# First-layer modulation weights loaded by column quarters, with the first products following the quarters

## The chip, the cores and the metric

The kernel runs on one core of one Trainium2 chip. The metric is the device time of one execution in microseconds (us). Three executions of the kernel before took 2706.11, 2706.01 and 2699.67 us; their median is 2706.01 us.

## The reference, cut to what matters

The network has two layers over a sequence of 2048 tokens of width 1024. Everything is float32. The first layer is a gated linear attention with four heads; before it, the input is normed and modulated by a condition vector `c`:

```
cond        = silu(c) @ w_ada[0] + b_ada[0]            # w_ada[0]: 1024 x 3072
shift, scale, gate = split(cond, 3)                    # 1024 each
h           = rms_norm(x, norm_gain[0]) * (1 + scale) + shift
q,k,v,g,lr  = split(h @ gla_w_in[0])                   # the first products
gk          = log_sigmoid(lr @ w_gk2 + b_gk) / 16      # the decay of each head
x           = x + gate * gla(q, k, v, g, gk) @ gla_w_out[0]
```

The second layer is a stick-breaking attention with sixteen heads whose keys and values come from the first layer's output; a last norm follows. The change touches only the calculation of `shift` and `scale` of the first layer and the first products that use them.

## The kernel before, in words

Channels lie on the 128 partitions and tokens along the free dimension. A block of 1024 channels is eight k-tiles (`KT` = 8), and the tokens are four groups of 512 (`TG`). Layer 0 goes over the groups (`layer0`). For each group it calculates `h` for eight k-tiles, and then for each head `v` (`pv`, two halves of two 128-token blocks), the key and the query (`pk`, `pq`), the decays (`gate`), the chunked attention (`gla`), and the output projection. A float32 value is held as a high and a low part in a form that TensorE multiplies in one pass, so each product is three matmuls: high by high, high by low, low by high. Weights are split the same way: ScalarE copies the high part (L116) and VectorE subtracts for the low part (L117).

TensorE's order is the order in which the program is written. The other engines are ordered by a planner, except in `start()`, which is written inside a region (L668) where TensorE, ScalarE, VectorE and SyncE all keep the written order too. The planner may put instructions of the rest of the program between those of the region.

`start()` is the work up to the first group's `h`. It loads `x` in four transfers and squares it on ScalarE; it loads `w_ada[0]`, columns 0 to 2047, as sixteen tiles of 128 rows by 1024 columns (`ada_rows`, L235), each multiplied by a column of silu(c) and added up on VectorE (L242, L244). Six of these come before the norm's `rstd` (L214) in VectorE's order and ten behind it. GpSimd multiplies `x` by `rstd` (L323). When all sixteen are added, TensorE sums them over partitions with sixteen one-column matmuls (L250), VectorE adds the bias and forms `1 + scale` times the gain (L331, L271), and for each k-tile `h` is scaled and shifted (GpSimd, VectorE or ScalarE, L338 and L341) and split (L230, L231). The split of the gate's low-rank weights (L371 to L375) and of the first `v` weights stands in front of that.

Behind `start()`, `gate_low_rank` (L378) multiplies each k-tile by the low-rank weights into `plr`, and the first half of the first head's `pv` runs between (L434 sorts it by k-tile). Its second half, `pk` and `pq` follow. The first head's `gate` is called four steps into what is left of `qkv`; it needs the finished `plr` (through `T.lr`), issues the matmul `u` (L395) and then a chain of VectorE and ScalarE instructions (L399 to L425), whose results are multiplied by `pk` (L457 to L460) and `pq` (L464, L465). The first attention matmul, `psc` (L474), needs the products of L457 and L464. It is written six steps behind the end of `qkv` of its head, between the `pv` matmuls of the next head.

Accumulation banks come from small pools: `pl` has four banks and holds `ms`, `plr`, `pv`, `pk`, `pq` and `u`; `pw` has two. The pool `act` has twelve tiles of 4 KB per partition (`w_ada` tiles and the first four k-tiles of `h` are among them), `wraw` three for unsplit weights and `wsp` ten for split ones.

Of the kernel before, what the change touches and what calls it, by code (L numbers as in the profile page):

```python
# [9 lines left out]
F32 = mybir.dt.float32  # L10
# [24 lines left out]
def yoco_kernel(ctx: ExitStack, tc: tile.TileContext, I: dict, O: dict):  # L35
# [29 lines left out]
    def bank(pool, name):  # L65
        return pool.tile([P, 512], F32, tag=pool.name, name=name)
# [241 lines left out]
    def start():  # L308

        T = start_group(0)  # L310
        w = I["w_ada"][0]
        rows = [ada_rows("l0", w, j, act) for j in range(2)]
        xs, sq = [], []
# [15 lines left out]
        for j in range(2):
            ada_sum(pc[:, 8 * j:8 * j + 8], accs[j])  # L330
        nc.vector.tensor_tensor(cond, pc[:, 0:16], b_ada[:, 0:16], op=ALU.add)  # L331
        a, b = mods["l0m"] = modulation("l0", norm_gain[:, 0:8], cond)
        xn = [t2(f"xn_0_{kt}") for kt in range(KT)]

        def scaled(kt):
            s, t = a[:, kt:kt + 1], b[:, kt:kt + 1]
            if kt % 2 == 0 and kt:
                nc.scalar.activation(xn[kt], xs[kt], AF.Identity, bias=t, scale=s)  # L338
            else:
                eng = nc.vector if kt < 1 else nc.gpsimd  # L340
                eng.tensor_scalar(xn[kt], xs[kt], s, t, op0=ALU.mult, op1=ALU.add)  # L341

        scaled(0)
        for kt in range(KT):
            if kt + 1 < KT:
                scaled(kt + 1)
            h = new_h(0, kt)
            T.hs.append(split(h[:, 0], h[:, 1], xn[kt]))
        return T
# [15 lines left out]

    def gate_weights():
# [3 lines left out]
        nc.sync.dma_start(raw2, I["w_gk2"])  # L370
        with urgent():  # L371
# [3 lines left out]
            nc.vector.tensor_tensor(gk2[64:96], raw2[64:96], gk2[64:96].bitcast(F32), op=ALU.subtract)  # L375

    def gate_low_rank(T):
        pr = bank(po, f"plr_{T.g}")  # L378
        for kt in range(KT):
            nc.tensor.matmul(pr[0:32], lrw[:, kt], T.hs[kt][0], start=kt == 0, stop=False)  # L380
            nc.tensor.matmul(pr[0:32], lrw[:, kt], T.hs[kt][1], start=False, stop=kt == KT - 1)
            yield
# [45 lines left out]
    def qkv(T, h):  # L428

        n = f"{T.g}_{h}"  # L430
        wv = next_weight()
        v = t4(f"v_{n}", [P, 4, GV])
        for half in range(2):
            pv = bank(pl, f"pv_{n}_{half}")  # L434

            steps = [(kt, s) for s in range(2) for kt in range(KT)]
            if T.g == h == half == 0:
                steps.sort()
            for i, (kt, s) in enumerate(steps):
# [9 lines left out]
            with urgent():  # L449
                nc.scalar.activation(v[:, 2 * half:2 * half + 2], pv, AF.Copy)  # L450
        wkq = next_weight()
        G = T.G[h]
        G.v = v
        pk = bank(pl, f"pk_{n}")
        yield from mm3(pk, wkq, 0, T.hs)
        with urgent():
# [3 lines left out]
            nc.vector.tensor_tensor(G.kf, pk, G.kf, op=ALU.mult)  # L460
        pq = bank(pl, f"pq_{n}")
        yield from mm3(pq, wkq, 1, T.hs)
        with urgent():
# [141 lines left out]
    def weight_blocks():  # L605

        for g in range(NG):
            seq = [("v", 0), ("kq", 0), ("v", 1), ("kq", 1), ("v", 2), ("kq", 2), ("g", 0),
                   ("v", 3), ("kq", 3), ("g", 1), ("g", 2), ("g", 3)] + [("out0", i) for i in range(4)]
            for kind, i in seq:  # L610
                yield load_split(f"{kind}{g}_{i}", I["w_" + kind][i])
# [49 lines left out]
    def layer0():  # L661
# [4 lines left out]
        for g in range(NG):  # L666
            T.ready = 0
            first = qkv(T, 0)  # L668
            for _ in gate_low_rank(T):
                if g == 0:  # L670
                    next(first)
            spawn(slow, 1, 9)
# [400 lines left out]
```

## Time and profile before

| | before |
|---|---|
| median of three executions | 2706.01 us |
| the profiled execution, its own time | 2703.88 us |
| its span, first to last instruction | 2702.1 us |
| mean granted clock of TensorE, as a share of full speed | 0.989 |
| TensorE busy | 2607.2 us, 96% |
| VectorE busy | 2110.4 us, 78% |
| ScalarE busy | 1517.6 us, 56% |
| GpSimd busy | 167.4 us, 6% |
| mean DMA rate | 138 GB/s |

The span runs from the first to the last instruction; 1.8 us of the execution's own time lie around it. PE is TensorE's matmuls, PEld its weight loads, DVE is VectorE, ACT is ScalarE, POOL is GpSimd and SPq is the queue of transfers that SyncE issues. Matmuls are pipelined, so one that the profile shows as 0.28 us long can be followed by the next after 0.12 us; the distance of starts is the pace. The granted clock of 0.50 is 1.2 GHz and 1.00 is 2.4 GHz.

### The profile page before, as it was taken

The page shows a single profiled execution, that of the slowest core. Times are in us where ns is not written, and L with a number is a line of the kernel's source. Part 1 is how long each engine was busy: PE and PEld are TensorE (multiplying, and loading weights), DVE is VectorE, ACT ScalarE, POOL GpSimd, SP SyncE. Part 2 cuts the span into 40 slices and gives each one's busy share as a digit, 9 for nine tenths or more (in the row PEclk, how much of TensorE's full clock was granted, in tenths as well). Part 3 has the DMA queues.
Part 4 walks back from the last instruction along what each step waited for, and adds up shares of the span by engine and source line. Part 5 has one row for each costly group of instructions (what it writes and reads, how often), then busy time and mean ns, then how long its engine had stood idle before and what let it go on. Part 6 is the DMA issues. An engine that isn't in the chain of part 4 may idle for free.

```text
span 2702.1 us, 38165 instructions
## 1 busy us (share of the span) xinstructions
PE 2607.2 (96%) x14040; PEld 2184.4 (81%) x14040; DVE 2110.4 (78%) x2933; ACT 1517.6 (56%) x2677; POOL 167.4 (6%) x358
## 2 busy tenths in 40 slices
PE   5999999999999999999999999999999999999998
PEld 4888888888788878788787887887887887887887
DVE  7647767676675658978979969979879789789866
ACT  4746756574485445545545645546556555556644
POOL 3000000000000011000010010010000010010000
PEclk7999999999999999999999999999999999999999
DMA  6326445545732463342243334243243243323464
GB/s 246 118 74 209 151 151 175 168 148 173 232 131 72 164 247 127 106 145 90 96 146 116 114 107 154 88 137 116 75 148 110 72 151 113 115 93 117 148 212 147
DMA packets 116682, 371.91 MB, mean 138 GB/s; under 512 B 13872, under 2 KB 18096, under 8 KB 116496
## 3 DMA queue, kind: packets, MB, share of 16 engines
q1 hardware_dynamic: 116496, 369.47, 40.8%
q8 instruction: 111, 1.82, 0.3%
q14 instruction: 75, 0.61, 0.1%
HBM read 311.75 MB, written 40.89 MB: 131 GB/s over the span
## 4 chain that ended last, share of the span: by engine, by line
PE 75%; DVE 17%; ACT 3%; issue 3%; DMA 1%; POOL 0%; SPq 0%; DVEq 0%; POOLq 0%; ACTq 0%
PE pt L838 7%; DVE S L830 5%; PE z L822 4%; PE o L856 4%; PE z L821 4%; PE o L855 3%; DVE sl L842 3%; PE pg L150 2%; PE pg L152 2%; PE pg L151 2%; PE pf L150 2%; PE pf L151 2%; PE pf L152 2%; PE py L150 2%; PE lk L150 2%
## 5 line engine op out<-in xcount | busy, mean ns | idle before, releaser
L841 ACT ACTIVATE sh<-pt 128x512 fp32r<-128x512 f32 (+3 forms) x640 | 341.5, 534 | 531.7 <-PE pt L838 522.1
L842 DVE SCALAR_TENSOR_TENSOR sl<-pt,sh 128x512 fp32r<-128x512 f32 (+3 forms) x640 | 384.0, 601 | 163.5 <-ACT sh L841 157.6
L830 DVE TENSOR_TENSOR_SCAN S<-S,S 128x512 f32<-128x512 f32 x384 | 489.5, 1275 | 3.4 <-ACT S L825 3.0
L838 PE MATMUL pt<-ident,S 128*128 128x128 f32 x2176 | 346.9, 275 | 34.7 <-DVE sl L842 34.2
L838 PEld LDWEIGHTS pt<-ident,S 128*128 128x128 f32 x2176 | 266.1, 141 | 119.7 <-DVE sl L842 33.0
L825 ACT ACTIVATE S<-z 128x512 f32<-128x512 f32 (+3 forms) x640 | 339.5, 531 | 12.6 <-PE o L856 4.6
L821 PE MATMUL z<-k,q 128*128 128x512 f32 (+3 forms) x640 | 284.4, 444 | 0.0
L822 PE MATMUL z<-k,ql 128*128 128x512 f32 (+3 forms) x640 | 234.1, 366 | 0.9 <-DVE sl L842 0.5
L856 PE MATMUL o<-sl,v 128*128 128x512 f32 (+3 forms) x640 | 234.2, 366 | 0.0
L855 PE MATMUL o<-sh,v 128*128 128x512 f32 (+3 forms) x640 | 230.6, 360 | 0.0
L830 DVE TENSOR_TENSOR_SCAN S<-S 128x128 f32<-128x128 f32 (+3 forms) x256 | 209.3, 820 | 19.7 <-POOL S L827 16.7
L827 POOL TENSOR_SCALAR_AFFINE_SELECT S<-S 128x128 f32<-128x128 f32 x256 | 86.1, 337 | 1251.1 <-ACT S L825 1232.2
L444 PE MATMUL pv<-wh_v,h 128*128 128x256 f32 x512 | 155.0, 303 | 0.0
L446 PE MATMUL pv<-wh_v,h 128*128 128x256 f32 x512 | 145.3, 284 | 0.0
L445 PE MATMUL pv<-wl_v,h 128*128 128x256 f32 x512 | 145.2, 284 | 0.0
L855 PEld LDWEIGHTS o<-sh,v 128*128 128x128 f32 x640 | 120.6, 188 | 27.2
L856 PEld LDWEIGHTS o<-sl,v 128*128 128x128 f32 x640 | 120.6, 189 | 25.7
L821 PEld LDWEIGHTS z<-k,q 128*128 128x128 f32 x640 | 121.8, 190 | 5.5
L822 PEld LDWEIGHTS z<-k,ql 128*128 128x128 f32 x640 | 123.1, 192 | 1.5 <-DVE sl L842 0.7
L150 PE MATMUL pg<-h,wh_g 128*128 128x512 f32 x256 | 112.6, 440 | 0.0
L150 PE MATMUL lk<-xb,wh_w_kv 128*128 128x512 f32 x256 | 102.5, 400 | 7.6 <-DVE oB L869 7.6
L150 PE MATMUL lv<-xb,wh_w_kv 128*128 128x512 f32 x256 | 102.9, 402 | 3.5 <-DMA xb<-xn 3.5
(266 smaller groups left out, 6350.3 us busy)
## 6 DMA issues: line engine op xcount, KB each, us to landing
xb<-xn SPq DMA_DIRECT2D x256, 512.0 KB, 5.0
wa_l<-in_w_ada_dram SPq DMA_DIRECT2D x40, 512.0 KB, 5.2
wr_f<-in_w_out_dram SPq DMA_DIRECT2D x40, 512.0 KB, 3.8
x<-in_x_dram SPq DMA_DIRECT2D x32, 512.0 KB, 6.5
wr_v<-in_w_v_dram SPq DMA_DIRECT2D x32, 512.0 KB, 4.5
wr_kq<-in_w_kq_dram SPq DMA_DIRECT2D x32, 512.0 KB, 4.1
wr_g<-in_w_g_dram SPq DMA_DIRECT2D x32, 512.0 KB, 3.9
wr_out<-in_w_out_dram SPq DMA_DIRECT2D x32, 512.0 KB, 3.8
```

The costliest lines, as they stand in the source:

```text
L150: nc.tensor.matmul(out, hi, x[kt][0], start=first and i == 0, stop=False)
L444: nc.tensor.matmul(o, xh, hi, start=i == 0, stop=False)
L446: nc.tensor.matmul(o, xl, hi, start=False, stop=i == len(steps) - 1)
L821: nc.tensor.matmul(z, L.q[:, h, tcol], k[:, h, 0:w], start=True, stop=False)
L822: nc.tensor.matmul(z, L.ql[h][:, tcol], k[:, h, 0:w], start=False, stop=True)
L825: nc.scalar.activation(s, z, AF.Sigmoid, scale=-SCALE_B)
L830: nc.vector.tensor_tensor_scan(s[:, ::-1], s[:, ::-1], s[:, ::-1], 1.0 if diag else self.before.S[tb][:, 0:1], ALU.mult, ALU.min)
L838: nc.tensor.transpose(pt[:, tb * P:(tb + 1) * P], self.S[tb][:, sb * P:(sb + 1) * P], ident)
L841: nc.scalar.activation(hi, pt[:, t0 * P:], AF.Copy, bias=-1.0)
L842: nc.vector.scalar_tensor_tensor(lo, pt[:, t0 * P:], -1.0, hi.bitcast(F32), op0=ALU.add, op1=ALU.subtract)
L855: nc.tensor.matmul(o, v, hi, start=self.diag and sb == 0, stop=False)
L856: nc.tensor.matmul(o, v, lo, start=False, stop=self.c == 0 and sb == 3)
```

## The change

`w_ada[0]`'s shift and scale columns now come in four quarters of 256 columns each: quarter `q` holds the 256 shift and the 256 scale columns that belong to k-tiles 2q and 2q+1. Each quarter is eight transfers of 128 rows by two pieces of 256 columns (256 KB each) into four tiles of `act`. For each quarter VectorE adds rows up for both halves over the first four row tiles (512 columns an instruction) and for the scale half alone over the last four (256 columns); TensorE multiplies the last four row tiles' shift halves by the silu column directly and adds them, with the sums, into one bank (12 one-column products). `scaled` multiplies `x` by `rstd` and the scale in one VectorE instruction and adds the shift on ScalarE, which writes the high part of `h`; `lows` writes the low part. GpSimd has no part any more.

For each quarter the first head's `pv` (both halves, `followers`) and `plr` follow for its two k-tiles, and from the second quarter on `pk` for the two k-tiles of the quarter before. The weights of the first `v` and of the first key and query are loaded and split inside `start()`. `qkv` of the first head then starts at `pq`, and `gate_low_rank` only finishes.

```diff
+        w = I["w_ada"][0][:, 0:2 * D].rearrange("(i a p) (j q c) -> q i p a j c", a=2, p=P, j=2, c=256)
...
+        def sums(q, kts):
+            if 0 in kts:
+                accs[q] = t2(f"aa_l0_{q}").rearrange("p (j c) -> p j c", j=2)
+            for kt in kts:
+                s, x, acc = s_col[:, kt:kt + 1], pieces[q][kt], accs[q]
+                if kt == 0:
+                    nc.vector.tensor_scalar(acc, x, s, None, op0=ALU.mult)
+                else:
+                    j = slice(0, 2) if kt < 4 else slice(1, 2)
+                    nc.vector.scalar_tensor_tensor(acc[:, j], x[:, j], s, acc[:, j], op0=ALU.mult, op1=ALU.add)
+
+        def products(q):
+
+            pc = bank(pw, f"pc_l0_{q}")[:, 0:4].rearrange("p (j f) -> p j f", j=2)
+            todo = [(0, f, pieces[q][kt][:, 0], s_col[:, kt:kt + 1]) for kt in range(4, KT) for f in range(2)]
+            todo += [(j, f, accs[q][:, j], ones) for j in range(2) for f in range(2)]
+            for i, (j, f, x, y) in enumerate(todo):
+                nc.tensor.matmul(pc[:, j, f:f + 1], x[:, f * P:(f + 1) * P], y, start=i == 0,
+                                 stop=i == len(todo) - 1)
+            return pc
...
+        load_ada(0)
+        lrs = gate_raws()
+        wv = halves("v", I["w_v"][0])
         r = rstd("x0", sq, mean_d)
...
+        for q in range(4):
+            if q == 0:
+                sums(0, range(KT))
+                pc = products(0)
+                conds(0, pc)
+                load_ada(1)
+            kts = 2 * q, 2 * q + 1
+            hs = [scaled(kt) for kt in kts]
+            if q == 0:
+                his(wv)
+                X.wv = los(wv)
+                gate_weights(*lrs)
+                wkq = halves("kq", I["w_kq"][0])
+            if q == 1:
+                his(wkq)
+                X.wkq = los(wkq)
+            if q < 3:
+                sums(q + 1, range(4))
+            for kt, x in zip(kts, hs):
+                lows(kt, *x)
+            if q < 3:
+                if q < 2:
+                    load_ada(q + 2)
+                sums(q + 1, range(4, KT))
+                pc = products(q + 1)
+                conds(q + 1, pc)
+            for kt in kts:
+                followers(kt)
+            if q:
+                run(mm3(X.pk, X.wkq, 0, T.hs, range(2 * q - 2, 2 * q), q == 1, False))
+        run(mm3(X.pk, X.wkq, 0, T.hs, range(6, 8), False, True))
         ahead.append(next(blocks))
...
+        if begun:
+            pk = begun.pk
+            pq = bank(pl, f"pq_{n}")
+            yield from mm3(pq, wkq, 1, T.hs)
```

## Rows read from the trace of the kernel before

**Rows 1.** The page's first part: busy time, share of the span and instructions of each engine.

```profile
PE 2607.2 (96%) x14040; PEld 2184.4 (81%) x14040; DVE 2110.4 (78%) x2933; ACT 1517.6 (56%) x2677; POOL 167.4 (6%) x358
```

**Rows 2.** The chain of work that ended last, in order of time: start, us, what. One of its early pieces.

```profile
5.89 9.66 PE ms_x L219 x16
```

**Rows 3.** VectorE's instructions in order of time, 0 to 50 us: start, us, engine, line, what, count, and in brackets the idle time before and what ended it.

```profile
18.90 0.75 DVE L225 SCALAR_TENSOR_TENSOR rq_x<-ms_x,epsc,rq_x 128x512 f32<-128x512 f32 x1 [0.31 <-ACT rq_x L224]
19.68 0.69 DVE L226 SCALAR_TENSOR_TENSOR r_x<-rq_x,r_x 128x512 f32<-128x512 f32 x1
20.30 3.48 DVE L244 SCALAR_TENSOR_TENSOR aa_l<-wa_l,s_col,aa_l 128x1024 f32<-128x1024 f32 x2
...
25.48 14.52 DVE L244 SCALAR_TENSOR_TENSOR aa_l<-wa_l,s_col,aa_l 128x1024 f32<-128x1024 f32 x7
39.91 0.28 DVE L373 TENSOR_TENSOR lrw<-lrw_raw,lrw 128x128 fp32r<-128x128 f32 x1
...
40.94 2.36 DVE L117 TENSOR_TENSOR wl_v<-wr_v,wh_v 128x1024 fp32r<-128x1024 f32 x2
43.66 0.17 DVE L331 TENSOR_TENSOR cond_l<-pc_l,vecs 128x16 f32<-128x16 f32 x1 [0.35 <-PE pc_l L250]
...
44.14 0.55 DVE L341 TENSOR_SCALAR xn<-x,a_l,cond_l 128x512 f32<-128x512 f32 x1
44.60 1.22 DVE L117 TENSOR_TENSOR wl_kq<-wr_kq,wh_kq 128x1024 fp32r<-128x1024 f32 x1
```

**Rows 4.** All engines in order of time: two of ScalarE's instructions, the same columns.

```profile
31.79 1.06 ACT L116 ACTIVATE wh_v<-wr_v 128x1024 fp32r<-128x1024 f32 x1 [0.37 <-DMA wr_v<-in_w_v_dram]
...
44.72 0.63 ACT L230 ACTIVATE h<-xn 128x512 fp32r<-128x512 f32 x1 [9.44 <-DVE xn L341]
```

**Rows 5.** TensorE's matmuls in order of time, the same columns: the first two products, three neighbours near 48.5 us and three near 54.8 us.

```profile
45.41 0.63 PE L380 MATMUL plr<-h,lrw 128*32 128x512 f32 x1 [1.78 <-ACT h L230]
...
46.89 0.63 PE L381 MATMUL plr<-h,lrw 128*32 128x512 f32 x1 [0.85 <-DVE h L231]
...
48.39 0.41 PE L446 MATMUL pv<-wh_v,h 128*128 128x256 f32 x1
...
48.60 0.63 PE L380 MATMUL plr<-h,lrw 128*32 128x512 f32 x1
...
49.03 0.63 PE L381 MATMUL plr<-h,lrw 128*32 128x512 f32 x1
...
54.69 0.28 PE L446 MATMUL pv<-wh_v,h 128*128 128x256 f32 x1
...
54.81 0.39 PE L380 MATMUL plr<-h,lrw 128*32 128x512 f32 x1
...
55.04 0.39 PE L381 MATMUL plr<-h,lrw 128*32 128x512 f32 x1
```

**Rows 6.** Stretches of the span: from and to, length, busy time of PE, PEld, DVE, ACT and POOL with instructions, the granted TensorE clock, the DMA share and GB/s.

```profile
17.00:18.00 1.00, 0.00 (x0) 0.00 (x0) 0.96 (x2) 0.99 (x2) 0.00 (x0) 0.90 1.03 422
...
24.00:27.00 3.00, 3.00 (x15) 3.00 (x16) 2.96 (x2) 0.00 (x0) 3.00 (x3) 0.50 1.02 418
...
40.00:44.00 4.00, 3.57 (x16) 3.48 (x16) 3.55 (x6) 0.00 (x0) 0.00 (x0) 0.50 0.20 55
...
51.00:52.00 1.00, 1.00 (x5) 0.74 (x4) 1.00 (x3) 1.00 (x2) 0.00 (x0) 0.53 0.00 0
```

**Rows 7.** TensorE's matmuls in order of time: the first head's `u`, the first and the last of its `pq`, and its first `psc`.

```profile
61.20 0.40 PE L395 MATMUL u<-lr,gk 96*128 96x512 f32 x1
...
70.02 0.40 PE L150 MATMUL pq<-h,wh_kq 128*128 128x512 f32 x1
...
75.25 0.39 PE L152 MATMUL pq<-h,wl_kq 128*128 128x512 f32 x1
...
81.23 0.39 PE L474 MATMUL psc<-e,gk 128*128 128x128 f32 x2
```

**Rows 8.** VectorE's and ScalarE's instructions in order of time, from the first head's `u` on: the chain's first and last, and some that stand between.

```profile
61.77 0.74 DVE L399 TENSOR_SCALAR gk<-u,vecs 128x512 f32<-128x512 f32 x1
...
63.13 1.05 ACT L116 ACTIVATE wh_v<-wr_v 128x1024 fp32r<-128x1024 f32 x1
...
64.61 0.58 ACT L450 ACTIVATE v<-pv 128x512 f32<-128x512 f32 x1
...
70.20 1.22 DVE L117 TENSOR_TENSOR wl_kq<-wr_kq,wh_kq 128x1024 fp32r<-128x1024 f32 x1
...
73.86 0.41 DVE L459 TENSOR_TENSOR kn<-pk,kn 128x256 f32<-128x256 f32 x1
...
74.20 0.62 ACT L422 ACTIVATE e<-e 128x512 f32<-128x512 f32 x1
...
79.53 0.68 DVE L464 SCALAR_TENSOR_TENSOR e<-pq,e 128x512 f32<-128x512 f32 x1
```

**Rows 9.** SyncE's transfers: in order of time the sixteen `w_ada` tiles, and from the list of DMA issues the eight reads of the last layer that come in pieces of 256 columns (KB each, median us from issue to landing).

```profile
3.11 16.73 SPq L239 DMA_DIRECT2D wa_l<-in_w_ada_dram  x16
...
x<-x SPq DMA_DIRECT2D x8, 256.0 KB, 5.3
```

**Rows 10.** Stretches again, the columns of rows 6: one in the middle of the first group; and from the list of who waited for whom (us in total, times, longest), the longest wait of TensorE in layer 0 behind 50 us.

```profile
100.00:200.00 100.00, 100.00 (x596) 86.68 (x595) 50.98 (x75) 53.20 (x79) 1.91 (x3) 1.00 0.23 73
...
PE psc L474 <- DVE e L464: 3.2, 2, 1.6
```

More of the change, by code (lines that the diff above doesn't have):

```diff
@@ L310, in start, with load_ada @@
         T = start_group(0)
-        w = I["w_ada"][0]
-        rows = [ada_rows("l0", w, j, act) for j in range(2)]
-        xs, sq = [], []
+        w = I["w_ada"][0][:, 0:2 * D].rearrange("(i a p) (j q c) -> q i p a j c", a=2, p=P, j=2, c=256)
+        cond = new_cond("l0", 2)
+        cj = cond.rearrange("p (j f) -> p j f", j=2)
+        ca = cpool.tile([P, KT], F32, tag="a_l0", name="a_l0")
+        mods["l0m"] = ca, cj[:, 0]
+        xs, sq, pieces = [], [], {}
+        def load_ada(q):
+            pieces[q] = []
+            for i in range(4):
+                raw = act.tile([P, 2, 2, 256], F32, tag="act", name=f"wa_l0_{q}_{i}")
+                for k in range(2):
+                    nc.sync.dma_start(raw[:, k], w[q, i][:, k])
+                pieces[q] += [raw[:, 0], raw[:, 1]]
@@ new lines, in lows, with halves, his, los @@
+        def lows(kt, xn, h):
+            nc.vector.scalar_tensor_tensor(h[:, 1], xn, cj[:, 0, kt:kt + 1], h[:, 0].bitcast(F32),
+                                           op0=ALU.add, op1=ALU.subtract)
+            T.hs.append((h[:, 0], h[:, 1]))
+        def halves(name, src):
+            return [load_half(f"{name}0_0", src, hf) for hf in range(2)]
+        def his(w):
+            for raw, hi, lo in w:
+                nc.scalar.activation(hi, raw, AF.Copy)
+        def los(w):
+            for raw, hi, lo in w:
+                nc.vector.tensor_tensor(lo, raw, hi.bitcast(F32), op=ALU.subtract)
+            return [(hi[:, j], lo[:, j]) for raw, hi, lo in w for j in range(4)]
@@ L314, in start @@
+        accs = {}
         for i in range(4):
@@ L329, in start @@
[L329 to L348, printed above, removed]
+        T.begun = Piece()
+        X = T.begun
+        X.pv = [bank(pl, f"pv_0_0_{half}") for half in range(2)]
+        T.pr = bank(po, "plr_0")
+        X.pk = bank(pl, "pk_0_0")
+        def followers(kt):
+            hi, lo = X.wv[kt]
+            for half in range(2):
+                for s in range(2):
+                    t0 = (2 * half + s) * P
+                    o = X.pv[half][:, s * GV:(s + 1) * GV]
+                    xh, xl = T.hs[kt][0][:, t0:t0 + P], T.hs[kt][1][:, t0:t0 + P]
+                    nc.tensor.matmul(o, xh, hi, start=kt == s == 0, stop=False)
+                    nc.tensor.matmul(o, xh, lo, start=False, stop=False)
+                    nc.tensor.matmul(o, xl, hi, start=False, stop=kt == KT - 1 and s == 1)
+            low_rank(T, kt)
@@ L375, in gate_weights, with low_rank @@
             nc.vector.tensor_tensor(gk2[64:96], raw2[64:96], gk2[64:96].bitcast(F32), op=ALU.subtract)
+    def low_rank(T, kt):
+        for i in range(2):
+            nc.tensor.matmul(T.pr[0:32], lrw[:, kt], T.hs[kt][i], start=kt == i == 0, stop=kt == KT - 1 and i == 1)
     def gate_low_rank(T):
[L378 to L382, printed above, removed]
+        if T.g:
+            T.pr = bank(po, f"plr_{T.g}")
+            for kt in range(KT):
+                low_rank(T, kt)
+        pr = T.pr
         T.lr = t2(f"lr_{T.g}", F32R)
@@ L430, in qkv @@
         n = f"{T.g}_{h}"
-        wv = next_weight()
+        begun = T.begun if T.g == h == 0 else None
+        wv = None if begun else next_weight()
         v = t4(f"v_{n}", [P, 4, GV])
         for half in range(2):
[L434 to L438, printed above, removed]
+            pv = begun.pv[half] if begun else bank(pl, f"pv_{n}_{half}")
+            steps = () if begun else [(kt, s) for s in range(2) for kt in range(KT)]
             for i, (kt, s) in enumerate(steps):
@@ L460, in qkv @@
             nc.vector.tensor_tensor(G.kf, pk, G.kf, op=ALU.mult)
-        pq = bank(pl, f"pq_{n}")
-        yield from mm3(pq, wkq, 1, T.hs)
+        if not begun:
+            pq = bank(pl, f"pq_{n}")
+            yield from mm3(pq, wkq, 1, T.hs)
         with urgent():
@@ L609, in weight_blocks @@
                    ("v", 3), ("kq", 3), ("g", 1), ("g", 2), ("g", 3)] + [("out0", i) for i in range(4)]
-            for kind, i in seq:
+            for kind, i in seq if g else seq[2:]:
                 yield load_split(f"{kind}{g}_{i}", I["w_" + kind][i])
@@ L668, in layer0 @@
             first = qkv(T, 0)
-            for _ in gate_low_rank(T):
-                if g == 0:
-                    next(first)
+            gate_low_rank(T)
             spawn(slow, 1, 9)
```

31 lines of the change are left out of this document (19 added, 12 removed).

## The prediction

> **What bounds the kernel now.** I read the page's busy shares first. TensorE is busy 96% of the span [rows 1], so what the change can give is what TensorE waits at the start, before its first product. The stretches say whether a gain or loss there would be swallowed later: between 100 and 200 us TensorE is busy all the time, and its longest wait in layer 0 behind the start is 3.2 us over two places [rows 10]. Nothing there swallows a shift of the start; it goes to the end one to one. So I compare one point of the program in both kernels: the first head's `psc`, reached at 81.23 us now [rows 7]. TensorE has the same products behind it in both.
>
> The chain of waits then shows what sets the start: `ms` first [rows 2], then `rstd` and the additions of `w_ada` on VectorE, until 40.0 us [rows 3]. The first product comes at 45.41 us [rows 5]. Two things in VectorE's list matter. Its last seven additions, over 1024 columns, take 2.07 us each (14.52/7) while GpSimd works beside them; `rstd`'s last step, over half as many columns before GpSimd begins, takes 0.69. And `rstd` leaves VectorE at 20.3 us [rows 3].
>
> **The change part by part.** VectorE keeps the written order, and `sums(0)` is written behind `rstd`. The six additions that VectorE does before `rstd` today have no counterpart: it idles until 18.9 us, and the whole rest stands in one line behind 20.3 us. Prices: an instruction over 512 columns that needs the one before it costs 0.72 us (0.69 and a step of 0.03), an independent one 0.62 us (19.68 to 20.30) [rows 3]; over 256 columns 0.43 us (0.41 and the step) [rows 8]; the first, single-input one of a quarter about 0.45 us (0.55 is the dearest near row [rows 3]). GpSimd is idle now, so I take none of them slowed.
>
> A quarter's sums: 0.45 + 3 x 0.72 + 4 x 0.43 = 4.3 us; the first four row tiles are 2.6 of them, the last four 1.7. The products' tail, behind the last sum, is two one-column products. Sixteen instructions of this kind took 3.57 us at the low clock, 0.22 us each [rows 6]; the two need four (a float32 product is two instructions), 0.9 us at the low clock and 0.5 at the high. The other ten products (twenty instructions, 4.5 us low, 2.2 high) lie beside VectorE's sums. `conds`: 0.5 us (43.66 to 44.14) [rows 3].
>
> VectorE's line, then:
> - 20.3 + 4.3 sums + 0.9 tail + 0.5 conds = 26.0; two `scaled`, 1.3: 27.3.
> - `los(wv)` must wait for ScalarE, which has two high parts of `h` (0.63 each) and then a copy of 1.06 us in front [rows 4]: 26.7 + 1.3 + 1.1 = 29.2. A stall of 1.9 us, then 2.4 us: 31.5. Gate weights, 1.0 us (39.91 to 40.94) [rows 3]: 32.5.
> - `sums(1)` 2.6, `lows` 1.3, the rest of `sums(1)` 1.7, tail 0.9: 38.8. Here the first followers start, 6.6 us before today's 45.41.
> - Second round: conds and scaled 1.8 (40.6), the same wait for ScalarE until 42.5, `los(wkq)` 2.4 (44.8), 2.6 + 1.3 + 1.7 + tail 0.9: 51.3. Followers of k-tiles 2 and 3 start.
> - Third round: 51.3 + 1.8 + 2.6 + 1.3 + 1.7 = 58.6, then the tail of `products(3)`.
>
> What stands behind these waits: on VectorE everything, so each of the four tails is on the path; on SyncE the second half of the key weights waits for `los(wv)` (30.4 us), and `load_ada(2)` and `load_ada(3)` behind it. Quarter 2 is wanted at 44.8 us. Today sixteen tiles of 512 KB are issued in 16.73 us, 1.05 us each; the reads in pieces of 256 columns took 5.3 us to land [rows 9]. Even if a 256 KB transfer took a whole turn of 1.25 us (512 KB at the 418 GB/s of rows 6), quarter 2's eight would be there at about 44. I cost the transfers at nothing, hidden beside VectorE; at two turns each they would be there at 54, and `sums(2)`, whose last part is wanted near 50, would lose some 4 us.
>
> TensorE's line: two k-tiles of followers are 24 `pv` and 4 `plr` matmuls. At the low clock these start 0.21 and 0.43 us apart, at the high one 0.12 and 0.23 [rows 5]: 6.8 or 3.8 us. The start at 38.8 is at the low one. Today the clock came back just before 52 us (0.53 on average over the stretch from 51) after TensorE had been at work without a gap from 46.9 [rows 5, 6], five us; with the same delay the first followers end at about 45. Then only one-column products come until 51.3. Is TensorE slow again by then? Today it fell to 0.90 on average between 17 and 18 us, soon after the `ms` matmuls ended at 15.5 [rows 2, 6], and the one-column products of 24 to 27 and 40 to 43.6 us ran at 0.50 throughout [rows 6]. I take it to be slow.
>
> The Trainium skill, page "TensorE: Matmul & The Clock Gate", section "HAM oscillation — how this bites in real kernels", says that a burst of matmuls shorter than the wait for the next data starts cold every time; it speaks against a start in four bursts. By it the second burst is slow, as I chose; rows 6 show the fall only behind an empty engine, not behind one-column products, and if these keep the clock up `pq` below starts at 70.4, not at 73.2.
>
> - Slow: followers 2 and 3 are 5.0 us at the low clock and the rest, 1.0, at the high, until 57.3; `pk` 0 and 1, six matmuls at 0.23 (a k-tile 0.68, (75.25 + 0.23 - 70.02)/8 [rows 7]), 1.4: 58.7; `products(3)`, queued behind them, 2.2 + 0.5: 61.4. VectorE waits 2.8 us for that. Then followers 3.8, `pk` 1.4, followers 3.8, `pk` 2.8: `pq` starts at 73.2.
> - Fast: the second tail takes 0.5, so the burst starts at 50.9 and is over at 56.1 with `pk`; `products(3)` waits for VectorE, 58.2, and ends at 58.6; the same 11.8 us more: 70.4.
>
> Today `pq` starts at 70.02 [rows 7]. So the early start is spent by the time `pk` ends.
>
> The second cost is the first head's `gate`. Today `u` is issued at 61.20 and hides behind half of `pv`, `pk` and `pq`; now only four k-tiles of `pq` stand in front of it and little behind. From `u` to the last exponential is 13.6 us today (61.20 to 74.82). Of this up to 2.8 us are other work in the way: a weight copy (1.05), the `v` copy (0.58), a low part (1.22) [rows 8]. Bounds: 10.8 and 13.6; such work will stand there again, so I take the middle, 12.2. Then L464, 0.68 us [rows 8]. `psc` may start 2.8 (four k-tiles) + 12.2 + 0.7 = 15.7 us behind the start of `pq`. In TensorE's order it comes 11.2 us behind (70.02 to 81.23 [rows 7]) plus two `u` of 0.23 us that are new in between: 11.7. So TensorE stalls 4.0 us. The next head's `u` falls into the same stall if it takes the bank of `pk`, which is read late in that chain; I count it once.
>
> Sum: 73.2 + 15.7 - 81.23 = +7.7 us. The profiled execution took 2703.88 us: 2711.6. It lies 2.1 us below the median of the three runs, inside their spread of 6.4 us. I predict 2712 us.
>
> About 0.3% (8.1 us) is what a measurement of this kernel can tell from no change. The forecast lies just inside it.
>
> **The rivals.**
> 1. Slower by more than that. One mechanism, `gate`'s chain standing bare: TensorE slow in the second burst (73.2), one weight split of 1.22 us slipped into the start as at 44.60 us today [rows 3], and the chain at its full 13.6 us. 74.4 + 17.1 - 81.23 = +10.3: 2714.2, and 2716 to 2720 where the planner puts more between. Point from which it decides: `psc` later than 89.3 us (81.23 + 8.1). For it: the planner did fill this chain today, and already at full cover `psc` waits for L464 twice, 3.2 us together [rows 10]. Against it: the weights of the next `v` are already split inside the start, so there is less left to fill with.
> 2. The clock stays high in the second burst and the chain is short: 70.4 + 14.3 - 81.23 = +3.5: 2707.4. For it: one-column products keep TensorE's loads busy [rows 6]. It is in the band of no change, as is the forecast.
> 3. Faster: the early start is kept. TensorE works from 38.8 us without a gap: 15.2 us of followers, 5.5 of `pk`, 5.4 of products (48 instructions at 0.11) and 3 lost to the low clock is 67.9; with `gate` hidden, 67.9 + 11.7 - 81.23 = -1.6: 2702.3. For more than 0.3% the planner's new order would have to save as much again several times later, and nothing in the rows points there.
>
> **How the numbers follow.** Forecast and rival 2 together 0.53, rival 1 0.38, rival 3 0.09. The forecast is itself near the edge, so part of it counts as slower and part of rival 1 and 3 as no change: faster 0.07, same 0.50, slower 0.43. The bounds alone give 2707.4 to 2714.2; with rival 3 below, the planner's fillings above and 3 us of spread between runs on either side, the range is 2701 to 2721.
>
> **What would show it.** First `pv` matmul at 37 to 41 us; VectorE idle until 18.9; a granted clock of 0.50 at 51 us; the last low part of `h` at 64 to 66 us (61 to 62 if the clock stays high); `pq` from 72 to 75 us; a wait of TensorE of 3 to 6 us for the first head's `gate`, at `psc` or the `u` before it; GpSimd without any work on `x`. Wrong would be: additions done before `rstd`; sums held up by transfers; `psc` before 82 us; or a time that moves by more than `psc` does.

## The result and the profile after

The changed kernel takes 2722.42 us (median of 6 runs, 2718.53 to 2724.57), the kernel before 2704.12 beside it: a ratio of 1.0067, 95% interval 1.0054 to 1.0080. It is slower by 18 us; 2712 was forecast, with a range up to 2721. The profiled execution of after took 2724.57 us, 20.7 more than that of before.

The page of after, first part; it answers to [rows 1]:

```profile
span 2722.8 us, 38338 instructions
PE 2624.1 (96%) x14104; PEld 2201.2 (81%) x14104; DVE 2108.3 (77%) x2962; ACT 1516.3 (56%) x2674; POOL 141.5 (5%) x346
```

Most of the additional time, 16.7 of the 20.7 us, arises where the prediction looked, and the shares hide it. TensorE's matmuls of after in order of time (answers to [rows 7]):

```profile
39.87 0.56 PE L403 MATMUL pv<-wh_v,h 128*128 128x256 f32 x1
...
76.16 0.39 PE L150 MATMUL pq<-h,wh_kq 128*128 128x512 f32 x1
...
78.89 0.39 PE L493 MATMUL u<-lr,gk 96*128 96x512 f32 x1
...
94.42 0.79 PE L576 MATMUL psc<-e,gk 128*128 128x128 f32 x2 [6.43 <-DVE e L566]
```

TensorE has its first follower at 39.9 us, 5.5 before the old first product, yet `pq` starts 6.1 us later than before (76.16 against 70.02) and `psc` 13.2 later (94.42 against 81.23). Behind it the distance still grows: 16.6 us at the first head's `ms_o` (128.3 against 111.7) and 16.7 at the first product of the output projection, `py` (243.0 against 226.3). `ms_o` of before, then of after:

```profile
111.67 1.02 PE L219 MATMUL ms_o<-ss_o,mean_v 128*128 128x512 f32 x2
```

```profile
128.27 1.12 PE L219 MATMUL ms_o<-ss_o,mean_v 128*128 128x512 f32 x2
```

VectorE in order of time, from its first sum of the change to the first head's `e` (answers to [rows 3] and [rows 8]):

```profile
19.93 0.48 DVE L334 TENSOR_SCALAR aa_l<-wa_l,s_col 128x512 f32<-128x512 f32 x1
20.45 4.41 DVE L337 SCALAR_TENSOR_TENSOR aa_l<-wa_l,s_col,aa_l 128x512 f32<-128x512 f32 x7
25.96 0.16 DVE L351 TENSOR_TENSOR cond_l<-pc_l,vecs 128x4 f32<-128x4 f32 x1 [1.11 <-PE pc_l L345]
...
29.51 2.36 DVE L377 TENSOR_TENSOR wl_v<-wr_v,wh_v 128x1024 fp32r<-128x1024 f32 x2 [1.73 <-ACT wh_v L373]
...
33.34 2.33 DVE L337 SCALAR_TENSOR_TENSOR aa_l<-wa_l,s_col,aa_l 128x512 f32<-128x512 f32 x3
35.58 1.41 DVE L364 SCALAR_TENSOR_TENSOR h<-xn,cond_l,h 128x512 fp32r<-128x512 f32 x2
36.91 2.04 DVE L337 SCALAR_TENSOR_TENSOR aa_l<-wa_l,s_col,aa_l 128x256 f32<-128x256 f32 x4
40.05 0.16 DVE L351 TENSOR_TENSOR cond_l<-pc_l,vecs 128x4 f32<-128x4 f32 x1 [1.10 <-PE pc_l L345]
...
43.64 2.36 DVE L377 TENSOR_TENSOR wl_kq<-wr_kq,wh_kq 128x1024 fp32r<-128x1024 f32 x2 [1.78 <-ACT wh_kq L373]
...
53.15 0.16 DVE L351 TENSOR_TENSOR cond_l<-pc_l,vecs 128x4 f32<-128x4 f32 x1 [1.10 <-PE pc_l L345]
...
63.02 0.16 DVE L351 TENSOR_TENSOR cond_l<-pc_l,vecs 128x4 f32<-128x4 f32 x1 [2.02 <-PE pc_l L345]
...
64.96 1.42 DVE L364 SCALAR_TENSOR_TENSOR h<-xn,cond_l,h 128x512 fp32r<-128x512 f32 x2
...
79.02 1.28 DVE L244 SCALAR_TENSOR_TENSOR aa_g<-wa_g,s_col,aa_g 128x1024 f32<-128x1024 f32 x1 [1.33 <-DMA wa_g<-in_w_ada_dram]
80.22 0.74 DVE L497 TENSOR_SCALAR gk<-u,vecs 128x512 f32<-128x512 f32 x1
...
88.38 1.28 DVE L244 SCALAR_TENSOR_TENSOR aa_g<-wa_g,s_col,aa_g 128x1024 f32<-128x1024 f32 x1
...
90.18 0.16 DVE L510 TENSOR_SCALAR bl<-b 128x4 f32<-128x4 f32 x1
...
93.68 0.69 DVE L566 SCALAR_TENSOR_TENSOR e<-pq,e 128x512 f32<-128x512 f32 x1
```

The four `cond_l` rows are the four tails: VectorE stands still before each, for TensorE's one-column products (`pc_l`) and not for a transfer. The two `wl` brackets are its waits for ScalarE's weight copies. The lower part is the gate's chain: two additions of the next modulation weights, `aa_g`, stand in it, one before L497 and one before L510. ScalarE in the same stretch has a third piece of other work, and then the chain's last exponential:

```profile
82.26 1.04 ACT L116 ACTIVATE wh_v<-wr_v 128x1024 fp32r<-128x1024 f32 x1
...
93.03 0.61 ACT L520 ACTIVATE e<-e 128x512 f32<-128x512 f32 x1
```

Stretches of after, the columns of [rows 6]; the third number from the end is the granted clock, 0.50 being 1.2 GHz and 1.00 being 2.4:

```profile
36.00:40.00 4.00, 1.73 (x9) 1.65 (x9) 2.84 (x6) 0.00 (x0) 0.00 (x0) 0.50 1.08 373
40.00:44.00 4.00, 4.00 (x19) 3.60 (x19) 2.10 (x5) 2.72 (x4) 0.00 (x0) 0.52 1.09 383
52.00:56.00 4.00, 3.90 (x17) 3.71 (x18) 2.79 (x7) 1.38 (x2) 0.00 (x0) 0.50 0.00 0
...
58.00:64.00 6.00, 6.00 (x46) 5.58 (x46) 3.81 (x9) 0.00 (x0) 0.00 (x0) 1.00 0.00 0
64.00:66.00 2.00, 2.00 (x11) 1.64 (x10) 1.87 (x4) 1.80 (x3) 0.00 (x0) 0.59 0.00 0
84.00:90.00 6.00, 4.00 (x33) 3.75 (x31) 5.18 (x7) 3.63 (x5) 0.00 (x0) 1.00 0.51 160
92.00:94.00 2.00, 0.00 (x0) 0.00 (x0) 1.54 (x4) 2.00 (x7) 0.00 (x0) 0.50 0.80 244
94.00:100.00 6.00, 5.58 (x23) 4.68 (x23) 3.98 (x6) 4.14 (x5) 0.00 (x0) 0.50 0.08 29
102.00:104.00 2.00, 2.00 (x18) 1.81 (x17) 0.11 (x1) 1.73 (x6) 0.64 (x1) 1.00 0.00 0
```

The last four are the new loss: TensorE runs out of work at 88, the clock falls while it waits, and from 94 to beyond 100 it works at 1.2 GHz. From `psc` to `ms_o` after takes 33.9 us and before, at 1.00 throughout, 30.4: that is the 3.4 us between `psc` (+13.2) and `ms_o` (+16.6).

### The profile page after: what moved, and what is told of

Same layout as the page of the kernel before. It is cut to its first block, busy times and chain, and to the rows that moved or that the text cites. A ratio compares the mean times of both kernels' runs of the same rounds, so it can differ in the third digit from the quotient of the medians.

```text
span 2722.8 us, 38338 instructions
## 1 busy us (share of the span) xinstructions
PE 2624.1 (96%) x14104; PEld 2201.2 (81%) x14104; DVE 2108.3 (77%) x2962; ACT 1516.3 (56%) x2674; POOL 141.5 (5%) x346
## 4 chain that ended last, share of the span: by engine, by line
PE 73%; DVE 16%; ACT 4%; issue 3%; DMA 2%; POOL 0%; SPq 0%; DVEq 0%; POOLq 0%; ACTq 0%
PE pt L939 7%; DVE S L931 5%; PE z L923 4%; PE o L957 4%; PE z L922 4%; PE o L956 3%; DVE sl L943 3%; PE pg L150 2%; PE pg L152 2%; PE pg L151 2%; PE py L150 2%; PE py L151 2%; PE lk L150 2%; PE lv L150 2%; PE py L152 2%
## 5 line engine op out<-in xcount | busy, mean ns | idle before, releaser
L540 PE MATMUL pv<-wh_v,h 128*128 128x256 f32 x480 | 147.6, 308 | 0.0
L542 PE MATMUL pv<-wh_v,h 128*128 128x256 f32 x480 | 137.4, 286 | 0.0
L541 PE MATMUL pv<-wl_v,h 128*128 128x256 f32 x480 | 137.3, 286 | 0.0
```

The costliest lines, as they stand in the source:

```text
L540: nc.tensor.matmul(o, xh, hi, start=i == 0, stop=False)
L542: nc.tensor.matmul(o, xl, hi, start=False, stop=i == len(steps) - 1)
```

## The experiments

Theory A, formed on this trace: the loss has three terms in series. VectorE's line makes `pq` late (6.1 us), the gate's chain behind `u` is not covered (6.4), and the low clock behind that wait costs again (3.4). Rival B: VectorE's line is all, and the wait only takes slack that was there. Rival C: the transfers of the quarters hold up the sums. All runs, with `pq`, `u`, `psc` (and TensorE's wait in front of it) and `py` by their first matmul in the profiled execution, in us:

| kernel | `pq` | `u` | `psc` (wait) | `py` | median, us | ratio to before [95%] |
|---|---|---|---|---|---|---|
| before | 70.0 | 61.2 | 81.2 (0) | 226.3 | 2702.4 to 2705.9 | 1 |
| after | 76.2 | 78.9 | 94.4 (6.4) | 243.0 | 2722.4 | 1.0067 [1.0054, 1.0080] |
| e1_gate_early | 75.6 | 75.3 | 91.8 (4.6) | 240.6 | 2716.9 | 1.0047 [1.0032, 1.0062] |
| e2_cover_back | 82.9 | 74.1 | 94.1 (0) | 239.2 | 2716.3 | 1.0040 [1.0025, 1.0055] |
| e3_sums_first | 69.7 | 72.4 | 88.1 (6.5) | 235.9 | 2716.0 | 1.0040 [1.0026, 1.0055] |
| e4_warm_start | 74.6 | 77.4 | 92.9 (6.5) | 240.8 | 2717.8 | 1.0049 [1.0034, 1.0064] |
| e5_filled_wait | 75.8 | 78.5 | 94.1 (1.0) | 240.9 | 2718.8 | 1.0051 [1.0036, 1.0066] |
| e6_his_early | 71.9 | 74.6 | 90.1 (6.4) | 238.7 | 2718.0 | 1.0048 [1.0033, 1.0064] |
| e7_twice | 76.0 | 78.7 | 94.6 (6.8) | 242.5 | 2721.1 (one run) | – |
| e8_urgent_gate | 75.7 | 78.4 | 93.9 (6.4) | 243.4 | 2721.6 | 1.0055 [1.0033, 1.0076] |
| e9_aa_later | 75.6 | 78.3 | 91.9 (4.5) | 241.1 | 2719.5 | 1.0062 [1.0048, 1.0075] |
| c1_four_moves | 66.1 | 65.8 | 79.6 (1.8) | 227.7 | 2706.2 | 1.0017 [1.0008, 1.0026] |
| c2_six_moves | 65.0 | 64.7 | 78.4 (1.8) | 227.5 | 2703.0 | 1.0000 [0.9991, 1.0009] |
| c3_six_and_fill | 63.7 | 63.4 | 77.2 (0) | 225.4 | 2704.0 | 0.9997 [0.9988, 1.0006] |

Two cautions. The intervals of the single moves reach into that of after or touch it, so by time alone only c1, c2 and c3 are told from after; what a single move does is read in the rows. And the rows jitter: VectorE's first instruction of `rstd` waits for ScalarE in every run, yet it starts anywhere from 17.97 us (e6) to 19.53 (e3), in after at 18.54. Shifts of up to 1.5 us are not told from that without taking it out.

**The gate earlier.** The first group's gate is emitted directly behind its low-rank part.

```diff
-            spawn(call(gate, T, 0), 3)
+            if g:
+                spawn(call(gate, T, 0), 3)
+            else:
+                gate(T, 0)
```

> One step is moved: the first head's gate is issued directly behind the finished plr, so u stands in front of pq and not behind four of its k-tiles. Theory A (the chain behind u stands bare, and TensorE's low clock after the wait costs more): u some 2.7 us earlier than its 78.9 us, psc at about 91.7 instead of 94.4, the wait in front of psc 3.7 instead of 6.4 us, total 2.7 us less, up to 6 if the clock no longer falls behind the shorter wait. Theory B (all of the loss is the late start of pq, set by VectorE's line in the start; the chain's place does not matter because other work would fill it): psc and total within 1 us of the changed kernel's.

`pq` comes 0.6 us earlier, `u` 3.6 and `psc` 2.6; from `u` to `psc` it is now 16.5 us instead of 15.5, so the wait falls to 4.6 and not to the expected 3.7. The median falls by 5.5 us, `py` by 2.4. A move that touches nothing of VectorE's line of sums brings `psc` forward as expected (91.8, expected 91.7), so B falls.

**The cover given back.** Half of `pv` and all of `pk` go back behind `u`, as in the kernel before.

```diff
-        X.pv = [bank(pl, f"pv_0_0_{half}") for half in range(2)]
+        X.pv = [bank(pl, "pv_0_0_0")]
...
-        X.pk = bank(pl, "pk_0_0")
...
-            for half in range(2):
+            for half in range(1):
...
-            if q:
-                run(mm3(X.pk, X.wkq, 0, T.hs, range(2 * q - 2, 2 * q), q == 1, False))
-        run(mm3(X.pk, X.wkq, 0, T.hs, range(6, 8), False, True))
...
+        pk = bank(pl, f"pk_{n}")
+        yield from mm3(pk, wkq, 0, T.hs)
```

> The quarters stay as they are, but the second half of the first head's pv and its pk go back behind start, as before the change; only the first half of pv and plr follow the quarters. Theory A: VectorE's line hardly changes (last low part of h near 65.5 us), u comes near 71 and its chain ends near 86 behind pv, pk and pq; no wait over 1 us at psc, psc near 90, the clock stays high behind it; 4 us from psc's place and 3.4 us from the clock, total about 7 to 8 us less than the changed kernel's 2722, so about 2714. Theory B: TensorE has done less work by the time the last low part is there, so everything comes later by what was moved out: psc not before 94, total the same or up to 4 us more.

`psc` of this kernel, and two of its stretches, with the columns of [rows 6]:

```profile
94.09 0.39 PE L567 MATMUL psc<-e,gk 128*128 128x128 f32 x2
```

```profile
60.00:68.00 8.00, 7.59 (x32) 6.80 (x33) 6.56 (x14) 1.38 (x2) 0.00 (x0) 0.50 0.02 8
72.00:94.00 22.00, 22.00 (x141) 19.99 (x140) 16.25 (x21) 17.61 (x29) 0.00 (x0) 1.00 0.48 158
```

No bracket: the wait is gone. But `psc` comes no sooner, where theory A had expected 90. The work kept back as cover has to be done behind the start, and with half the followers in the start the clock stayed at 0.50 from 52 to 68 us; the run does not part the two. What is gained lies behind: `psc` at the same time, `py` 3.8 us earlier, where TensorE reaches `psc` at 2.4 GHz and takes 30.4 us from there to `ms_o`, as before did. That is the third term without the second.

**The wait filled.** 24 products that nothing reads in front of the first `psc`.

```diff
+        if T.g == h == 0:
+            fill = bank(pz, "fill")
+            x = T.hs[0][0]
+            for _ in range(24):
+                nc.tensor.matmul(fill, x[:, 0:P], x, start=True, stop=True)
         psc = bank(pw, f"psc_{n}")
```

> 24 extra products of 512 columns (0.23 us each, 5.5 us, into a bank of their own that nothing reads) are issued in TensorE's order directly in front of the first head's psc, in the place where TensorE waits 6.4 us. Theory A: psc stays at 94.4 us, the granted clock stays at 1.00 from 88 to 102 us where it was 0.50 from 92 to 102, and the total falls by about 3.4 us. Theory B: the low clock there costs nothing that reaches the end, total unchanged or up to 1 us more.

```profile
88.00:102.00 14.00, 13.00 (x83) 11.05 (x82) 10.07 (x17) 11.18 (x25) 0.29 (x1) 1.00 0.23 76
```

`psc` stays at 94.1, the clock at 1.00 through the wait, and the median falls by 3.7 us (within the intervals) though nothing useful was done. In the profiled execution `py` gains 2.1 only, since `ms_o` then waits 1.4 us for VectorE.

**Quarter 0 summed ahead of `rstd`**, as VectorE's idle time up to 18.5 us invites.

```diff
         wv = halves("v", I["w_v"][0])
+        sums(0, range(KT))
         r = rstd("x0", sq, mean_d)
...
             if q == 0:
-                sums(0, range(KT))
```

> The sums of quarter 0 are written in front of rstd in VectorE's order, so they run beside the landing of quarter 0 between 10 and 16 us instead of at 20 to 25. Theories A and B alike: VectorE's line in the start moves forward by 5 to 6 us (first conds near 20.1 instead of 26.0), the last low part of h near 61, psc near 89, total 5 to 6 us less than the changed kernel. Theory C (the transfers in pieces of 256 columns hold up the sums): the later sums then wait for landings, and less than 2 us of it arrives.

`psc` moves by 6.3 us, `py` by 7.1, the median by 6.4. The wait at `psc` stays at 6.5: the two terms are in series.

**Weights' high parts ahead of `h`'s** on ScalarE, which takes away the two waits for `wh_v` and `wh_kq`.

```diff
         r = rstd("x0", sq, mean_d)
+        his(wv)
...
-                his(wv)
                 X.wv = los(wv)
...
+                his(wkq)
             if q == 1:
-                his(wkq)
                 X.wkq = los(wkq)
```

> ScalarE's high parts of the v and key weights are written ahead of the high parts of h, so that VectorE does not wait for them (two waits of 1.7 and 1.8 us). VectorE's line then ends 3.5 us sooner (last low part of h at 62.9 instead of 66.4 us), pq near 73, psc near 91, total 3 to 4 us less by theories A and B. By theory C (transfers) the low parts would wait for the weights' landing instead, and less than 1 us arrives.

`pq` and `psc` move by 4.3 us, the median by 4.4. Of that 0.6 is the earlier `rstd` of this execution (17.97 against 18.54); the rest, 3.7, is about the two waits (3.5).

**Warm followers.** 20 wide products that nothing reads among the one-column ones.

```diff
+                if (q, i) in WN:
+                    for _ in range(WN[q, i]):
+                        nc.tensor.matmul(fill, T.hs[0][0][:, 0:P], T.hs[0][0], start=True, stop=True)
                 nc.tensor.matmul(pc[:, j, f:f + 1], x[:, f * P:(f + 1) * P], y, start=i == 0,
...
+        WN = {(2, 8): 6, (2, 10): 10, (3, 10): 4}
```

> 20 extra products of 512 columns (into a bank that nothing reads) are put between the one-column products of quarters 2 and 3, where TensorE waits for VectorE's sums; the rest is the changed kernel. Theory A (the bursts of the start run at the low clock because only one-column products stand between them): the granted clock stays at 1.00 from 46 us on, the second and third burst take 3.8 instead of 6.4 and 5.4 us, pq starts near 72.5 instead of 76.2, psc near 91, total 3 to 4 us less than the changed kernel. Theory B (VectorE's line alone sets pq): pq moves by less than 1 us, total unchanged.

A burst here is the followers of one quarter, run without a gap. The second burst ran at 1.00 throughout, but the clock fell at the third instead (0.64 from 60 to 64 us). `pq` gains 1.6 us, where theory A had expected 3.7. The low clock in the start is a small term here, and these products only moved it to another burst.

**Each quarter transferred twice**, the copies into tiles that nothing reads.

```diff
+            for i in range(4):
+                again = m4.tile([P, 2, 2, 256], F32, tag="m4", name=f"again_{q}_{i}")
+                for k in range(2):
+                    nc.sync.dma_start(again[:, k], w[q, i][:, k])
```

> Each of the 32 transfers of 256 KB is issued a second time into tiles that nothing reads, behind its quarter: 8 MB more in the same 50 us. Theories A and B (transfers are hidden beside VectorE's line): psc within 1 us of 94.4, no wait of VectorE for a transfer of over 0.5 us. Theory C (transfers in small pieces set the start): the sums of quarters 1 to 3 wait, and psc comes 5 us later or more.

TensorE's waits in its first 100 us: who waited for whom, us in total, times, longest.

```profile
PE psc L580 <- DVE e L570: 6.8, 1, 6.8
...
PE pc_l L349 <- DMA wa_l<-in_w_ada_dram: 0.8, 1, 0.8
```

The 0.8 us lie at the second quarter's first products (27.5), beside VectorE's sums; VectorE waits for no quarter. Doubling the bytes moves `psc` by 0.2 us. C falls.

**The gate by priority**, and **the next modulation weights' additions later.**

```diff
+    def urgent_gate(T, h):
+        with urgent():
+            gate(T, h)
...
-            spawn(call(gate, T, 0), 3)
+            spawn(call(urgent_gate if g == 0 else gate, T, 0), 3)
```

```diff
-            spawn(slow, 1, 9)
+            spawn(slow, 1 if g else 30, 9)
```

> The first head's gate keeps its place, but the planner is told to put its instructions ahead of weight splits and additions for later. Theory A (other work in the chain is part of the wait): from u to the last exponential 11 to 12.5 instead of 14.75 us, the wait at psc 3 to 4.5 instead of 6.4 us, total 2.5 to 5 us less. Theory B: psc and total within 1 us of the changed kernel.

> The additions for the layer's gate vector (1.28 us each on VectorE), four of which stand in the first head's chain, are spawned 30 steps later; nothing else is changed. Theory A (other work stands in the chain behind u): gone are 0.75 us in front of the chain's first instruction and 1.2 us in front of L510; u to last exponential 12.5 to 13 instead of 14.75 us, psc 92 to 92.7 instead of 94.4, total 2 to 4 us less. Theory B': the chain is as long as its own instructions and the planner's weight splits fill the gaps: psc within 0.7 us.

VectorE under the gate by priority:

```profile
79.12 1.28 DVE L244 SCALAR_TENSOR_TENSOR aa_g<-wa_g,s_col,aa_g 128x1024 f32<-128x1024 f32 x1 [0.78 <-DMA wa_g<-in_w_ada_dram]
80.32 0.75 DVE L497 TENSOR_SCALAR gk<-u,vecs 128x512 f32<-128x512 f32 x1
...
88.49 1.28 DVE L244 SCALAR_TENSOR_TENSOR aa_g<-wa_g,s_col,aa_g 128x1024 f32<-128x1024 f32 x1
89.68 0.16 DVE L510 TENSOR_SCALAR bl<-b 128x4 f32<-128x4 f32 x1
```

Priority did nothing for this chain: the same two `aa_g` stand at the same places, so this run missed what it was to show. Spawning them later takes them out (e9), and `psc` comes 2.5 us earlier. Of this 0.6 is there at `u` already, in a start that ran earlier. The rest, 1.9 us, is not simply the two additions, as VectorE and ScalarE of e9 show:

```profile
78.75 0.75 DVE L497 TENSOR_SCALAR gk<-u,vecs 128x512 f32<-128x512 f32 x1 [2.95 <-PE u L493]
...
85.97 1.22 DVE L117 TENSOR_TENSOR wl_v<-wr_v,wh_v 128x1024 fp32r<-128x1024 f32 x1
```

```profile
82.20 0.63 ACT L500 ACTIVATE e<-e 128x512 f32<-128x512 f32 x1
82.74 1.04 ACT L116 ACTIVATE wh_v<-wr_v 128x1024 fp32r<-128x1024 f32 x1
```

L497 follows `u` (78.31) after 0.4 us instead of 1.3: that is the first addition. The weight copy `wh_v` now stands behind L500 and no longer in front of it, another 0.9. In the place of the second addition the planner put a weight split of the same length, L117, so nothing is gained there; that is what theory B' had said of every gap. By the ratio (1.0062 against 1.0067) the run is not told from after.

**Moves together.** c1 joins e1, e3, e6 and e9. c2 adds two: the low parts of `h` go behind the next quarter's sums, and 22 wide products stand among the one-column ones.

```diff
-            for kt, x in zip(kts, hs):
-                lows(kt, *x)
             if q < 3:
...
                 sums(q + 1, range(4, KT))
                 pc = products(q + 1)
+            for kt, x in zip(kts, hs):
+                lows(kt, *x)
+            if q < 3:
                 conds(q + 1, pc)
```

> Four single moves together: quarter 0's sums ahead of rstd, the weights' high parts ahead of h, the gate directly behind plr, the gate vector's additions later. Alone they brought psc 6.3, 4.3 and 2.6 us forward, the last is expected to bring 2. If they add up (they act on VectorE's line and on the chain, one behind the other): pq near 65.5, psc near 79.5 against 81.2 in the kernel before, wait at psc under 2 us with the clock at 1.00 behind it, total within 3 us of the kernel before (ratio 0.999 to 1.001). If TensorE's own work in the cold start becomes the bound instead, pq not before 68 and the total 3 to 6 us above before.

> The four moves and two more: the low parts of h are written behind the sums of the next quarter, so that VectorE does not wait for the one-column products (1.1 us at each of three places), and 22 extra wide products stand in TensorE's waits between the one-column ones of quarters 2 and 3, to hold the clock. Expected against the four moves: VectorE's line 2 to 3 us shorter, bursts at the high clock, pq 2 to 4 us sooner, total 2 to 4 us less, so 0 to 4 us below the kernel before (ratio 0.9985 to 1.000). If the extra products stand in the way instead of in waits: the same as the four moves or up to 2 us more.

`psc` is now ahead of before by 1.6 and 2.8 us, yet c1 is slower by 0.17% and c2 equal. c2's `pq` comes 1.1 us ahead of c1's, where 2 to 4 had been expected. A stretch of c2, which had run at 1.00 from 40 to 80 us:

```profile
80.00:84.00 4.00, 4.00 (x19) 3.34 (x18) 0.98 (x2) 3.92 (x5) 0.00 (x0) 0.51 0.00 0
```

Behind a wait of only 1.8 us at `psc` the clock fell, and the lead was spent. So a last run filled that wait with 9 products.

```diff
+            for _ in range(9):
+                nc.tensor.matmul(fill, x[:, 0:P], x, start=True, stop=True)
         psc = bank(pw, f"psc_{n}")
```

> The six moves, and 9 more products of 512 columns that nothing reads, on a bank of their own, in front of the first head's psc (added work). In the six moves alone psc comes at 78.4 us, 2.8 us ahead of the kernel before, behind a wait of 1.8 us, and TensorE's clock is 0.51 at 80 to 84 us and 0.63 at 84 to 88; the first py then comes at 227.5, 1.2 us behind the kernel before. Theory A (a wait costs its own length and the low clock behind it): 9 products of about 0.22 us fill the 1.8 us, psc stays at 78.2 to 79.0, the clock at 80 to 88 is 1.00, the first py comes at 223.5 to 225, and the time is 2.5 to 4 us below the six moves alone, a ratio to the kernel before of 0.9980 to 0.9992. Rival (the loss after psc in the six moves comes from the order of VectorE's and ScalarE's work behind the first head and not from the clock): py stays at 227 to 228 and the ratio at 1.000.

The clock stays at 1.00 and `psc` comes at 77.2, 4.1 us ahead of before. This execution's `rstd` was 0.95 us ahead of c2's (18.49 against 19.44) and its `u` 1.4; counted from `u`, `psc` comes as in c2 (13.8 us against 13.7), which is what theory A said of the fill. But `py` is ahead of before by only 0.9, at 225.4 where 223.5 to 225 was expected, and the ratio is 0.9997 where 0.9980 to 0.9992 was: theory A holds at `psc` and misses behind it, where the rival had put the loss. TensorE and VectorE of c3 show where the lead went:

```profile
110.65 1.13 PE L219 MATMUL ms_o<-ss_o,mean_v 128*128 128x512 f32 x2 [2.89 <-DVE ss_o L204]
```

```profile
105.42 1.29 DVE L244 SCALAR_TENSOR_TENSOR aa_g<-wa_g,s_col,aa_g 128x1024 f32<-128x1024 f32 x1 [0.26 <-DMA wa_g<-in_w_ada_dram]
106.62 0.69 DVE L572 SCALAR_TENSOR_TENSOR e<-pq,e 128x512 f32<-128x512 f32 x1
...
109.91 0.68 DVE L204 TENSOR_TENSOR ss_o<-ss_o,sq_o 128x512 f32<-128x512 f32 x1
```

and VectorE of the kernel before:

```profile
106.15 0.68 DVE L464 SCALAR_TENSOR_TENSOR e<-pq,e 128x512 f32<-128x512 f32 x1
...
108.48 0.68 DVE L204 TENSOR_TENSOR ss_o<-ss_o,sq_o 128x512 f32<-128x512 f32 x1
```

Against a lead of 4.1 us at `psc`, VectorE reaches the second head's `e` 0.5 us later than before and `ss_o` 1.4 later, and TensorE waits 2.9 us for it. With the start faster, VectorE's line in the second head is what ends last. One of the `aa_g` additions that e9's move sent later stands directly in front of that `e` (105.42, 1.29 us), where before has none: part of the lead went into the work that had been moved away. No run without it was made. No version beat the kernel before by more than its interval.

## Why the prediction was wrong

What held: VectorE idle to 18.54; first followers at 40; GpSimd without work on `x`; transfers hidden; VectorE's two stalls for ScalarE (1.73 and 1.78 us, 1.9 predicted); 0.50 at 51 us and into the second burst; a stall at `psc`. Just outside their ranges lie the last low part (done at 66.4, predicted 64 to 66), `pq` (76.2, 72 to 75) and the wait at `psc` (6.4, 3 to 6). By its deciding point, `psc` later than 89.3, it was rival 1 that came true, and beyond its 2716 to 2720: TensorE slow in the second burst and the chain bare, as it said, but no weight split slipped into the start.

The direction and the two terms of the sum were right; their sizes failed, and a third term was missing. By its own sum, 73.2 + 15.7 - 81.23 = +7.7 (its list of VectorE's line comes to 39.0 where it says 38.8, 32.5 + 6.5; nothing hangs on that):

- **VectorE's line**, too short. The sum over 256 columns was priced 0.43 us from a row of other work [rows 8]; it takes 0.51 (2.04/4). Three over 512 were 2.16; they take 2.24 (33.34 to 35.58). The tail was 0.9; it takes 1.1. Each is small, but all stand in one line: first followers 1.1 us late (39.87 against 38.8), the second burst 1.7 (52.97 against 51.3).
- **"Slow" in the second burst alone.** The third was taken at the high clock; part of it ran low too, 0.59 from 64 to 66 us and 0.56 from 66 to 68. In the repeats of this start with other edits (e1, e7, e8) the second burst stayed low longer and the third ran at 1.00, and `pq` came at 75.6 to 76.0 all the same. Both terms together: `pq` at 76.16 instead of 73.2.
- **The gate's chain**, taken as 12.2 us with 13.6 as upper bound. It took 14.75 (78.89 to the end of the exponential at 93.64), above the bound: the bound was the first head's chain of the kernel before, which had other work in it, and the planner put more into this one. e9 shows what can be taken out: 0.9 us for the addition ahead of L497 and 0.9 for the weight copy ahead of L500, and its chain takes 12.8. The wait was 6.4 us instead of 4.0.
- **A missing term: what a wait does to the clock behind it.** The wait was priced by its length, and the low clock behind it at nothing, without a reason. It cost 3.4 us more from `psc` to `ms_o`. e2, without the wait, takes as long there as before and gives back 3.8 us at `py`; e5, with the wait filled, gives back 2.1 and loses 1.4 to VectorE.

With the measured sizes, 2.73 from `pq` to `u`, 14.75 and 0.78 from there to `psc`, 18.26 in all, the same formula gives 76.16 + 18.26 - 81.23 = +13.2, which is the shift of `psc` and so only sorts it into terms, and +16.6 with the missing term. The prediction had named it as a sign of error that the time moves by more than `psc` does, and it did: 18.

The rest, 1.6 us by the medians and 4.0 by the profiled executions, lies behind `py`, and I could not isolate it. From the first `py` to the second layer's first `lv`, before takes 726.6 us and after 728.6. In all fourteen profiled executions this length goes with the low clock in it: (1 - granted clock) x 4 us, added over stretches of 4 us, gives 0 in c2 (723.4 us long), 3.3 in before, 6.8 in after and 8.6 in e8 (733.0); the length is 723 us and this sum, to within 2 us. No run tested which sets which. The other 2.0 us of the profiled difference lie behind `lv`. The first `psc` of the second group shows how little decides it; before, and then after:

```profile
305.49 0.49 PE L474 MATMUL psc<-e,gk 128*128 128x128 f32 x2 [1.62 <-DVE e L464]
```

```profile
322.06 0.49 PE L576 MATMUL psc<-e,gk 128*128 128x128 f32 x2 [1.55 <-DVE e L566]
```

The same wait, but only after's clock fell there, to 0.50 at 325 to 329 us. Why it falls at one such wait and not at another is open. It also limits what medians say: c3's `py` leads c2's by 2.1 us, and its median does not.

The Trainium skill's rule weighed in the prediction (page "TensorE: Matmul & The Clock Gate", section "HAM oscillation — how this bites in real kernels": a burst shorter than the wait for its data starts cold each time) agrees with the second burst, at 0.50 from 52 to 56 us. As put here it does not reach the wait at `psc`, in front of which TensorE had worked without a gap from 53 to 88 us; that the clock was at 0.50 from 94 to 100 us behind this wait is shown by the trace.

## What to carry to other kernels

Work taken from behind a long chain and put ahead of it is not free when the engine is idle there: it was the chain's cover. Before moving work forward, write down the chain that it hid, at its full length with the other work that the planner puts into it, and price the uncovered part twice: its length, and the lower clock behind it. And when several such terms stand in series, removing one showed nearly its size at `psc` here (2.6 us in e1, 6.3 in e3, 4.3 in e6), but once all are gone the next engine's line (here VectorE in the second head) takes over within a few us.

## What the runs showed of the hardware that was not expected

- TensorE's clock fell while it was busy: without a gap from 58 to 66 us, on wide products, then from 60.25 on the one-column products of the last quarter and from 62.85 on wide ones again, it was at 1.00 up to 64 us and at 0.59 on average from 64 to 66.
- Behind a wait of TensorE of 1.8 us the clock fell to 0.51 (c2, 80 to 84 us), and with 9 products in its place it stayed at 1.00 (c3). At the second group's first `psc` it fell behind a wait of 1.55 us in after and not behind one of 1.62 in before.
- Transfers of 256 KB in pieces of 1 KB went at 373 GB/s in a stretch in which SyncE had issued nothing else for 5 us (36 to 40 us of after); 512 KB in larger pieces went at 418 from 24 to 27 us of before [rows 6] and at 384 from 27 to 30. Twice as many of the small ones were hidden as well (e7).
